# Two lines on when the last gate's steps are handed out: credit reset without pending work, and one more step between cast and sum

## The chip, the cores and the metric

The kernel runs on one core of a Trainium2 chip. The metric is the device time of one execution in microseconds (us). Of the engines, PE (TensorE) multiplies matrices, DVE (VectorE) and ACT (ScalarE) do element-wise work, POOL (GpSimd) does a few small operations, and SP (SyncE) issues the DMA transfers. Each engine works its own queue in order, and engines wait for one another by semaphores.

## The reference

One block of a diffusion transformer on 512 tokens of `x` and 256 of a context, width 1024, all in float32. Nine modulation vectors come from `c`, and three sublayers follow: a SwiGLU feed-forward (ffn1), a mixer of windowed attention and a gated scan, and a second SwiGLU feed-forward (ffn2). Each is normalized, shifted and scaled before, and gated behind. What matters here:

```python
mod = (silu(c) @ w_ada + b_ada).reshape(B, 9, 1, D)      # m[j] = mod[:, j]
h = ada_pre(x, norm_pre[2], m[6], m[7])
x = x + 0.5 * m[8] * rmsnorm(swiglu(h, ffn2_w_in, ffn2_w_out), norm_post[2])
```

`m[8] * norm_post[2] * 0.5` is called the last gate below. It is wanted only at the very end of ffn2, where the result is normalized and added.

## The kernel before, in words

Every matrix product is done in three passes: each operand is split into a rounded part (an ACT cast, line 65) and the remainder (a DVE subtraction, line 66), and PE multiplies high by high, low by high and high by low. So each weight tile costs an ACT cast and a DVE subtraction before PE can use all of it.

**ffn2** (`ffn7`) runs over 22 tiles j of 128 hidden columns. Tiles 0 and 1 are computed in the plain way (`std_tile`), tiles 2 to 21 by a scheme with seven products instead of eight: `weights(j)` loads two raw tiles U and G (512 KB each) through a pool of three buffers `wraw`, forms three sums on DVE (lines 408 to 411), and splits four stationary operands g0, g2, g1 and gc (`wh`/`wl`, three buffers, and `wch`/`wcl`, one). The seven products are twelve matmuls each, in the order A = g0, B = g0's other half, A = g2, C = g1, A += gc, C += g2, A += g1. Between uses, A and C are taken out of PSUM by ACT (lines 476, 483, 485, 492) and DVE (478, 487, 489). PE can start the last product of a tile only when DVE's line 487 has read A. Tiles are grouped into pieces of 1, 3, 3, 3, 3, 3, 2 and 4; after the first tile of a piece, PE multiplies the piece before it by the output weights (lines 71 to 74 with `woh`, the output phase).

**The modulation work** beside it is a list of generators, `background`. `mod_half` computes 512 columns of `silu(c) @ w_ada`: eight times it loads 256 KB of `w_ada` into `wa` (two buffers) and lets DVE multiply and add it into `macc` (lines 611 and 613), yielding its cost after each. Then it splits `macc` (the cast and remainder into `mx`, two buffers) and lets PE sum over the partitions with a stationary operand of ones (lines 622 and 623, an `aux` bank of PSUM). `mod_gate` does this for two halves, and behind each sum loads a row of `b_ada` and one of `norm_post` into the same `mx` buffers and combines them (lines 656 and 657).

**What hands the steps out** is `tick(n)` (line 294). It adds n to a credit, and runs steps of `background` while the credit is above zero; each step subtracts what it yields. ffn1 calls it 42 times with 4.2 (176.4 in all) and once with 1000 at its end. Its four generators yield 32, 64, 16 and 32, which is 144, so the credit stands at over 1000 when ffn2 begins. ffn2 puts the last gate's generator on the list at the end of tile 1 (line 1198) and calls `tick(1)` twice in each of the tiles 2 to 21.

The program text written this way is then put in a fixed order for each engine by the Tile framework's scheduler, which looks ahead by its own costs. So the order of the rows below is that of the built program, not that of the source.

Of the kernel before, what the change touches and what calls it, by code (L numbers as in the profile page):

```python
# [37 lines left out]
def view(ap, off, dims):  # L38

    return AP(ap.tensor, ap.offset + off, [ap.ap[0]] + [list(d) for d in dims])  # L40
# [3 lines left out]
def kernel(ctx: ExitStack, tc: tile.TileContext, i, out):  # L44
# [10 lines left out]
    def ps(tag="mm", shape=(P, 512)):  # L55
        return psum.tile(list(shape), F32, tag=tag, name=nm(tag), bufs=4)

    def ct(shape, tag, dt=F32, bufs=1, pool=None):
        return (pool or core).tile(list(shape), dt, tag=tag, name=nm(tag), bufs=bufs)

    def f32(ap):
        return ap.bitcast(F32)

    def split(hi, lo, src):
        nc.scalar.copy(hi, src)  # L65
        nc.vector.tensor_tensor(out=lo, in0=src, in1=f32(hi), op=ALU.subtract)  # L66
# [73 lines left out]
    def make_cols(n, v, shift, scale):  # L140

        a = ct([P, KD], f"colA{n}{v}")
        b = ct([P, KD], f"colB{n}{v}")
        jb, js = 3 * n, 3 * n + 1
        nc.vector.tensor_tensor(out=b, in0=shift, in1=vec[:, R_B + jb * KD:R_B + (jb + 1) * KD], op=ALU.add)
        nc.vector.tensor_tensor(out=a, in0=scale, in1=vec[:, R_B + js * KD:R_B + (js + 1) * KD], op=ALU.add)
        nc.vector.scalar_tensor_tensor(out=a, in0=a, scalar=1.0, in1=vec[:, R_PRE + n * KD:R_PRE + (n + 1) * KD],
                                       op0=ALU.add, op1=ALU.mult)
        mcol[n, v] = lambda k: (a[:, k:k + 1], b[:, k:k + 1])
# [65 lines left out]
    def rstd(z, n, scratch):  # L215

        ss = ct([P, 1], "ss", bufs=8)
        if isinstance(z, (list, tuple)):
            s2 = ct([P, 2], "ss2", bufs=4)
            for q, zz in enumerate(z):  # L220
                nc.scalar.activation(scratch[:, q * 512:(q + 1) * 512], zz, AF.Square, accum_out=s2[:, q:q + 1])
            nc.vector.tensor_tensor(out=ss, in0=s2[:, 0:1], in1=s2[:, 1:2], op=ALU.add)
        else:
            nc.scalar.activation(scratch, z, AF.Square, accum_out=ss)
        r = ct([P, 1], "rs", bufs=8)
        nc.gpsimd.tensor_scalar(ss, ss, 1.0 / n, EPS, ALU.mult, ALU.add)  # L226
        nc.gpsimd.tensor_tensor(out=r, in0=ss, in1=mhalf, op=ALU.pow)  # L227
        return r
# [61 lines left out]
    background = []  # L290

    credit = [0.0]

    def tick(n):

        credit[0] += n
        while background and credit[0] > 0:
            try:
                credit[0] -= next(background[0])
            except StopIteration:  # L300
                background.pop(0)
# [299 lines left out]
    with tc.tile_pool(name="f1", bufs=1, reuse_waits="tile") as f1:  # L601

        def mod_half(j, h, vs, pool):

            accs = [ct([P, 512], "macc", bufs=2, pool=pool) for _ in vs]
            for k in range(KD):
                w = ct([P, 512], "wa", bufs=2, pool=pool)
                nc.sync.dma_start(w, i["w_ada"][0, k * P:(k + 1) * P, j * D + h * 512:j * D + (h + 1) * 512])
                for v, a in zip(vs, accs):
                    if k == 0:  # L610
                        nc.vector.tensor_scalar(a, w, cs[:, v, k:k + 1], None, ALU.mult)
                    else:
                        nc.vector.scalar_tensor_tensor(out=a, in0=w, scalar=cs[:, v, k:k + 1], in1=a,  # L613
                                                       op0=ALU.mult, op1=ALU.add)
                yield len(vs)
            outs = []
            for v, a in zip(vs, accs):
                o = ps("aux")
                hi = ct([P, 512], "mx", F32R, bufs=2, pool=pool)
                lo = ct([P, 512], "mx", F32R, bufs=2, pool=pool)  # L620
                split(hi, lo, a)
                nc.tensor.matmul(o, lhsT=ones, rhs=hi, start=True, stop=False)
                nc.tensor.matmul(o, lhsT=ones, rhs=lo, start=False, stop=True)
                outs.append(o)
            return outs

        def mod_cols(n, vs, pool):
            cols = {(j, v): ct([P, KD], "mc", bufs=4, pool=pool) for j in range(2) for v in vs}
            for j in range(2):
                for h in range(2):  # L630
                    outs = yield from mod_half(3 * n + j, h, vs, pool)
                    for v, o in zip(vs, outs):
                        m = ct([P, 512], "mx", bufs=2, pool=pool)
                        nc.vector.tensor_tensor(out=m.rearrange("p (a b) -> p a b", b=P),
                                                in0=o.rearrange("p (a b) -> p a b", b=P),
                                                in1=view(ident, 0, [(0, 4), (1, P)]), op=ALU.mult)
                        nc.vector.tensor_reduce(out=cols[j, v][:, h * 4:(h + 1) * 4],
                                                in_=m.rearrange("p (a b) -> p a b", b=P), axis=AX.X, op=ALU.add)
            for v in vs:
                make_cols(n, v, cols[0, v], cols[1, v])  # L640

        def mod_gate(n, vs, w, pool):
            j = 3 * n + 2
            for v in vs:
                gg[n, v] = ct([P, D], "gg", bufs=3)
            for h in range(2):
                cols = slice(h * 512, (h + 1) * 512)
                outs = yield from mod_half(j, h, vs, pool)
                bb = ct([P, 512], "mx", bufs=2, pool=pool)
                b_, np_ = i["b_ada"], i["norm_post"]  # L650
                nc.sync.dma_start(bb, AP(b_.tensor, b_.offset + j * D + h * 512, [[0, P], [1, 512]]))
                gb = ct([P, 512], "mx", bufs=2, pool=pool)
                nc.sync.dma_start(gb, AP(np_.tensor, np_.offset + n * D + h * 512, [[0, P], [1, 512]]))
                for v, o in zip(vs, outs):
                    g = gg[n, v][:, cols]
                    nc.vector.tensor_tensor(out=g, in0=o, in1=bb, op=ALU.add)
                    nc.vector.scalar_tensor_tensor(out=g, in0=g, scalar=float(w), in1=gb, op0=ALU.mult, op1=ALU.mult)

        hh2 = ct([P, KD, TA], "hh", F32R)
        hl2 = ct([P, KD, TA], "hl", F32R)  # L660
        waiting = {}
        hts = []

        def post(t, o, n, v, w4, res):

            y = tok[t]
            scr = ct([P, D], "w4", bufs=4, pool=w4)
            for h in range(2):
                hc = slice(h * 512, (h + 1) * 512)
                nc.vector.tensor_tensor(out=y[:, hc], in0=y[:, hc], in1=o[h], op=ALU.add)  # L670
            r = rstd(y, D, ct([P, D], "am", mybir.dt.bfloat16, bufs=2, pool=w4))
            nc.vector.tensor_tensor(out=scr, in0=y, in1=gg[n, v], op=ALU.mult)
            nc.vector.scalar_tensor_tensor(out=y, in0=scr, scalar=r, in1=res, op0=ALU.mult, op1=ALU.add)
            return scr

        def last1(t, o):
            res = ct([P, D], "wraw", bufs=3)
            src = i["x"][0, t * P:(t + 1) * P, :] if t < NX else i["ctx"][0, (t - NX) * P:(t - NX + 1) * P, :]
            nc.sync.dma_start(res, src)
            scr = post(t, o, 0, 0 if t < NX else 1, f1, res)  # L680
            waiting[t] = pre_xn(t, scr)
            for s in sets:
                if t == s[-1]:
                    hts.append(make_hT(1, hh2, hl2, s, [waiting[q] for q in s], f1, tag="sg"))
            steps(hts, HT_STEPS.get(t, 0))

        for t in range(NT):
            tok[t] = ct([P, D], "tok", bufs=6)
        background += [mod_gate(0, (0, 1), 0.5, f1), mod_cols(1, (0, 1), f1),
                       mod_gate(1, (0,), 1.0, f1), mod_cols(2, (0,), f1)]  # L690
        first_w = []

        def final_pre():
            first_w.append(v_w(0))

        ffn(i["ffn1_w_in"][0], i["ffn1_w_out"][0], (hh, hl), GROUPS, NT, f1, PIECES, tok, last1,
            pre=pre1, ticks=4.2, final_pre=final_pre, order=ORDER)
        steps(hts, 1000)
# [223 lines left out]
    with tc.tile_pool(name="ma", bufs=1, reuse_waits="tile") as ma:  # L922
# [42 lines left out]
        vs = ct([P, NT, 2, 2, 64], "vs", F32R, pool=ma)  # L965
# [298 lines left out]
```

## Time and profile before

| | us |
|---|---|
| time, median of 3 runs (1508.75 to 1509.24) | 1508.85 |
| the profiled execution | 1511.06 |
| its span | 1509.3 |
| PE busy in the span | 1433.2 (95%) |
| DVE busy in the span | 984.5 (65%) |
| ACT busy in the span | 583.2 (39%) |

The span is what the trace covers, from its first instruction to its last. The profiled execution has 1.8 us around it. ffn1 fills about the first 610 us, and the mixer what lies between it and ffn2, whose first tiles begin at about 1130 us; tile 2 begins at 1152 us. A matmul's own duration in a timeline is longer than its distance to the next, since matmuls are pipelined; so a row of PE is read by its start.

### The profile page before, as it was taken

How to read it: one execution, taken by the hardware profiler on the slowest of the kernel's cores; microseconds unless marked ns; L12 is line 12 of the kernel's file. 1: busy time of each engine (PE TensorE's matmuls, PEld its weight loads, DVE VectorE, ACT ScalarE, POOL GpSimd, SP SyncE). 2: the span in 40 equal slices, each digit the busy share in tenths (PEclk: the TensorE clock that was granted, in tenths of full speed). 3: DMA queues.
4: the chain of work that ended last, by engine and by line, in shares of the span. 5: the costliest groups of instructions: out<-in, count | busy, mean ns of one | idle time of the engine just before them, and what ended most of it. 6: DMA issues, size and time to landing. Idle time of an engine off the chain costs nothing.

```text
span 1509.3 us, 22491 instructions
## 1 busy us (share of the span) xinstructions
PE 1433.2 (95%) x9064; PEld 1228.2 (81%) x9064; DVE 984.5 (65%) x1601; ACT 583.2 (39%) x973; POOL 59.2 (4%) x87
## 2 busy tenths in 40 slices
PE   6999999999999999899999899999996699999997
PEld 3688888888788887789889677788776599999996
DVE  6866564666654334856687679743468677787785
ACT  6532121212121122532333578632256244454442
POOL 3200000000000000200001100000010000000001
PEclk9999999999999999999999999999999799999999
DMA  9554332455551111221121111133316333333311
GB/s 309 177 187 132 105 113 80 121 162 152 169 154 42 56 43 56 80 85 43 43 68 52 56 43 57 32 99 100 117 46 213 108 102 106 101 101 109 95 47 56
DMA packets 177904, 151.57 MB, mean 100 GB/s; under 512 B 6408, under 2 KB 152328, under 8 KB 177800
## 3 DMA queue, kind: packets, MB, share of 16 engines
q1 hardware_dynamic: 177800, 150.14, 32.8%
q8 instruction: 71, 1.16, 0.3%
q14 instruction: 33, 0.27, 0.1%
HBM read 148.02 MB, written 2.10 MB: 99 GB/s over the span
## 4 chain that ended last, share of the span: by engine, by line
PE 68%; issue 15%; DVE 7%; DMA 4%; ACT 3%; POOL 2%; SPq 0%; DVEq 0%; POOLq 0%; ACTq 0%
PE mm L71 17%; PE mm L74 16%; PE mm L72 16%; DMA wa<-w_ada 3%; PE mm L421 2%; PE mm L422 2%; PE mm L423 2%; PE aux L421 2%; PE aux L422 2%; PE aux L423 2%; DVE macc L613 1%; POOL rs L227 1%; DVE wl L66 1%; PE aux L1044 1%; POOL ss L226 1%
## 5 line engine op out<-in xcount | busy, mean ns | idle before, releaser
L71 PE MATMUL mm<-hh,wh 128*128 128x512 f32 (+1 forms) x1128 | 388.9, 346 | 0.5 <-ACT sg L332 0.2
L72 PE MATMUL mm<-hl,wh 128*128 128x512 f32 (+1 forms) x1128 | 368.0, 343 | 0.0
L74 PE MATMUL mm<-hh,wl 128*128 128x512 f32 (+1 forms) x1128 | 325.5, 346 | 0.7 <-DVE wl L66 0.7
L66 DVE TENSOR_TENSOR wl<-wraw,wh 128x1024 fp32r<-128x1024 f32 (+1 forms) x159 | 189.5, 1196 | 179.2 <-ACT wh L65 178.0
L65 ACT CAST wh<-wraw 128x1024 fp32r<-128x1024 f32 (+1 forms) x159 | 163.1, 1028 | 355.5 <-PE mm L72 230.6
L71 PEld LDWEIGHTS mm<-hh,wh 128*128 128x128 f32 x1128 | 212.1, 188 | 46.0 <-ACT gg L909 0.7
L72 PEld LDWEIGHTS mm<-hl,wh 128*128 128x128 f32 x1128 | 212.4, 188 | 27.2 <-DVE hl L541 0.8
L74 PEld LDWEIGHTS mm<-hh,wl 128*128 128x128 f32 x1128 | 185.6, 190 | 8.9 <-DVE wl L66 1.1
L71 PE MATMUL mm<-woh,acth 128*128 128x512 f32 x420 | 164.5, 392 | 1.9 <-DVE am L334 1.1
L72 PE MATMUL mm<-wol,acth 128*128 128x512 f32 x420 | 164.0, 391 | 0.0
L613 DVE SCALAR_TENSOR_TENSOR macc<-wa,cs,macc 128x512 f32<-128x512 f32 x140 | 101.8, 749 | 61.7 <-DMA wa<-w_ada 60.7
L74 PE MATMUL mm<-woh,actl 128*128 128x512 f32 x420 | 130.6, 390 | 0.0
L65 ACT CAST woh<-w 128x1024 fp32r<-128x1024 f32 x42 | 44.3, 1055 | 153.5 <-PE mm L74 150.7
L71 PEld LDWEIGHTS mm<-woh,acth 128*128 128x128 f32 x420 | 78.9, 188 | 20.0 <-DVE am L334 2.0
L74 PEld LDWEIGHTS mm<-woh,actl 128*128 128x128 f32 x420 | 78.8, 188 | 16.6
L72 PEld LDWEIGHTS mm<-wol,acth 128*128 128x128 f32 x420 | 78.9, 188 | 15.6
L369 DVE TENSOR_TENSOR tok<-tok,mm 128x512 f32<-128x512 f32 x96 | 61.5, 683 | 34.5 <-PE mm L74 34.4
L421 PE MATMUL mm<-hh,wh 128*128 128x256 f32 x240 | 68.1, 284 | 2.0 <-ACT up L476 2.0
L421 PE MATMUL aux<-hh,wh 128*128 128x256 f32 x240 | 69.1, 288 | 0.0
L422 PE MATMUL aux<-hl,wh 128*128 128x256 f32 x240 | 69.0, 287 | 0.0
L423 PE MATMUL aux<-hh,wl 128*128 128x256 f32 x240 | 68.9, 287 | 0.0
L423 PE MATMUL mm<-hh,wl 128*128 128x256 f32 x240 | 67.8, 283 | 0.1
(342 smaller groups left out, 2478.5 us busy)
## 6 DMA issues: line engine op xcount, KB each, us to landing
wraw<-ffn_w_in SPq DMA_DIRECT2D x88, 512.0 KB, 4.0
wa<-w_ada SPq DMA_DIRECT2D x128, 256.0 KB, 3.2
w<-ffn_w_out SPq DMA_DIRECT2D x44, 512.0 KB, 4.3
wraw<-mix_w_in SPq DMA_DIRECT2D x42, 512.0 KB, 3.7
tok<-w_ada SPq DMA_DIRECT2D x16, 256.0 KB, 5.6
wraw<-w_out SPq DMA_DIRECT2D x8, 512.0 KB, 4.3
tok<-x SPq DMA_DIRECT2D x4, 512.0 KB, 8.2
wraw<-x SPq DMA_DIRECT2D x4, 512.0 KB, 3.3
```

What stands on the lines that cost most here:

```text
L65: nc.scalar.copy(hi, src)
L66: nc.vector.tensor_tensor(out=lo, in0=src, in1=f32(hi), op=ALU.subtract)
L71: nc.tensor.matmul(o, lhsT=sh, rhs=mh, start=start, stop=False)
L72: nc.tensor.matmul(o, lhsT=sh, rhs=ml, start=False, stop=False)
L74: nc.tensor.matmul(o, lhsT=sl, rhs=mh, start=False, stop=stop)
L226: nc.gpsimd.tensor_scalar(ss, ss, 1.0 / n, EPS, ALU.mult, ALU.add)
L227: nc.gpsimd.tensor_tensor(out=r, in0=ss, in1=mhalf, op=ALU.pow)
L369: nc.vector.tensor_tensor(out=y, in0=y, in1=o[h], op=ALU.add)
L421: nc.tensor.matmul(o, lhsT=wk, rhs=mh, start=first and k == 0, stop=False, skip_group_check=True)
L422: nc.tensor.matmul(o, lhsT=wk, rhs=ml, start=False, stop=False, skip_group_check=True)
L423: nc.tensor.matmul(o, lhsT=wl[:, k0 + k, :], rhs=mh, start=False, stop=k == H4 - 1, skip_group_check=True)
L613: nc.vector.scalar_tensor_tensor(out=a, in0=w, scalar=cs[:, v, k:k + 1], in1=a, op0=ALU.mult, op1=ALU.add)
```

## The change

Two places. In `tick`, the credit is set to zero whenever the list of pending work is empty, so that what ffn1 did not use is not carried to ffn2. In `mod_half`, where one vector is computed and not two (`len(vs) == 1`), one more step of cost 1 is yielded between the split and the sum by PE. That concerns the last gate, and in ffn1 the two generators with one vector (`mod_gate(1, ...)` and `mod_cols(2, ...)`, six halves).

```diff
     def tick(n):
 
-        credit[0] += n
+        credit[0] = credit[0] + n if background else 0.0
         while background and credit[0] > 0:
...
                 split(hi, lo, a)
+                if len(vs) == 1:
+                    yield 1
                 nc.tensor.matmul(o, lhsT=ones, rhs=hi, start=True, stop=False)
                 nc.tensor.matmul(o, lhsT=ones, rhs=lo, start=False, stop=True)
```

From line 622 on, a line of the new kernel has a number two higher. In the rows of the built programs a name carries a buffer number, and an arrow points from what is read to what is written.

On PE, in tile 2 of ffn2, the rows before from the last matmuls of the product gc (`wch`) on; `ones` is the sum over partitions of a half of the last gate, `aux_10489` the second product B:

```order
L421 MATMUL mm_10488<-hh_9717,wch_10472 128x256
L422 MATMUL mm_10488<-hl_9718,wch_10472 128x256
L423 MATMUL mm_10488<-hh_9717,wcl_10473 128x256
L622 MATMUL aux_10412<-mx_10413,ones_62 128x512
L623 MATMUL aux_10412<-mx_10414,ones_62 128x512
L622 MATMUL aux_10450<-mx_10451,ones_62 128x512
L623 MATMUL aux_10450<-mx_10452,ones_62 128x512
L421 MATMUL aux_10489<-hh_9717,wh_10467 128x256
L422 MATMUL aux_10489<-hl_9718,wh_10467 128x256
```

The same place now, from the last matmuls of gc on:

```order
L421 MATMUL mm_10416<-hh_9717,wch_10400 128x256
L422 MATMUL mm_10416<-hl_9718,wch_10400 128x256
L423 MATMUL mm_10416<-hh_9717,wcl_10401 128x256
L421 MATMUL aux_10448<-hh_9717,wh_10406 128x256
L422 MATMUL aux_10448<-hl_9718,wh_10406 128x256
L423 MATMUL aux_10448<-hh_9717,wl_10407 128x256
L421 MATMUL aux_10448<-hh_9717,wh_10406 128x256
L422 MATMUL aux_10448<-hl_9718,wh_10406 128x256
L423 MATMUL aux_10448<-hh_9717,wl_10407 128x256
```

The four matmuls with `ones` are gone from tile 2; B now stands ahead of gc, and behind gc comes C += g2 of the same tile.

They now stand in tile 6 (the first half; `wh_11035` is g0 of tile 6, `wh_11046` its g2) and, for the second half, in tile 11 behind an output phase:

```order
L423 MATMUL aux_11057<-hh_9717,wl_11036 128x256
L421 MATMUL aux_11057<-hh_9717,wh_11035 128x256
L422 MATMUL aux_11057<-hl_9718,wh_11035 128x256
L423 MATMUL aux_11057<-hh_9717,wl_11036 128x256
L624 MATMUL aux_11026<-mx_11027,ones_62 128x512
L625 MATMUL aux_11026<-mx_11028,ones_62 128x512
L421 MATMUL mm_11056<-hh_9717,wh_11046 128x256
L422 MATMUL mm_11056<-hl_9718,wh_11046 128x256
```

On DVE, behind the split of tile 2's weights, before (`macc` is the last gate's accumulator, `wraw_10590` U of tile 3):

```order
L408 TENSOR_TENSOR wc_10598<-wraw_10590,wraw_10592 128x512
L409 TENSOR_TENSOR wraw_10592<-wraw_10592 128x512
L613 SCALAR_TENSOR_TENSOR macc_10387<-wa_10400,cs_75,macc_10387 128x512
L66 TENSOR_TENSOR wcl_10600<-wc_10598,wch_10599 128x512
L613 SCALAR_TENSOR_TENSOR macc_10387<-wa_10403,cs_75,macc_10387 128x512
L613 SCALAR_TENSOR_TENSOR macc_10387<-wa_10406,cs_75,macc_10387 128x512
L613 SCALAR_TENSOR_TENSOR macc_10387<-wa_10409,cs_75,macc_10387 128x512
L66 TENSOR_TENSOR mx_10414<-macc_10387,mx_10413 128x512
L611 TENSOR_SCALAR macc_10425<-wa_10426,cs_75 128x512
L613 SCALAR_TENSOR_TENSOR macc_10425<-wa_10429,cs_75,macc_10425 128x512
```

And now, where `wraw_10524` is U of tile 3:

```order
L489 TENSOR_TENSOR up_10418<-up_10418,aux_10448 128x256
L409 TENSOR_TENSOR wraw_10526<-wraw_10526 128x512
L66 TENSOR_TENSOR wcl_10534<-wc_10532,wch_10533 128x512
L493 TENSOR_TENSOR up_10418<-sg_10449,up_10418 128x512
L410 TENSOR_TENSOR wraw_10524<-wraw_10524,wraw_10526 128x512
L613 SCALAR_TENSOR_TENSOR macc_10387<-wa_10672,cs_75,macc_10387 128x512
L66 TENSOR_TENSOR actl_10518<-up_10418,acth_10517 128x512
L411 TENSOR_TENSOR wraw_10524<-wraw_10524 128x512
L478 TENSOR_TENSOR up_10551<-up_10551,aux_10550 128x256
L613 SCALAR_TENSOR_TENSOR macc_10387<-wa_10729,cs_75,macc_10387 128x512
L66 TENSOR_TENSOR wl_10540<-wraw_10524,wh_10539 128x1024
```

Before, the sixteen multiplications by `w_ada` stood almost one behind another ahead of tile 2's line 478. Now they stand singly or in twos between the tiles' own work, the first five ahead of tile 3's remaining splits and the last one ahead of tile 6's first sum.

On SP, the transfers of `w_ada` (`wa`) and of the weights (`wraw`) moved in the same way. Now, from the load of G of tile 3 (`wraw_10526`) on:

```order
L96 DMA wraw_10526<-ffn_w_in 128x8x128
L608 DMA wa_10672<-w_ada 128x512
L96 DMA wraw_10675<-ffn_w_in 128x8x128
L608 DMA wa_10729<-w_ada 128x512
L345 DMA w_1989_11675<-ffn_w_out 128x1024
L608 DMA wa_10893<-w_ada 128x512
L608 DMA wa_10950<-w_ada 128x512
L96 DMA wraw_10677<-ffn_w_in 128x8x128
L96 DMA wraw_10896<-ffn_w_in 128x8x128
```

## Rows read from the trace of the kernel before

**Rows 1.** The page: granted TensorE clock in 40 slices, tenths.
```profile
PEclk9999999999999999999999999999999799999999
```

**Rows 2.** Windows: us, busy PE, PEld, DVE, ACT, POOL, PEclk, DMA.
```profile
1150.00:1160.00 10.00, 7.32 (x46) 6.11 (x45) 8.65 (x10) 6.15 (x10) 0.00 (x0) 1.00 0.80 243
1160.00:1170.00 10.00, 0.00 (x0) 0.00 (x0) 4.99 (x7) 1.15 (x2) 0.00 (x0) 0.75 0.78 247
1170.00:1180.00 10.00, 1.52 (x2) 0.57 (x2) 4.72 (x8) 0.09 (x1) 0.00 (x0) 0.50 0.59 182
...
1190.00:1200.00 10.00, 10.00 (x75) 9.80 (x75) 7.91 (x12) 5.69 (x9) 0.00 (x0) 0.89 0.09 22
```

**Rows 3.** Waits of PE, 1100 to 1290 us: total us, times, longest us.
```profile
PE aux L622 <- ACT mx L65: 24.4, 2, 14.2
PE mm L421 <- ACT up L476: 2.0, 1, 2.0
...
PE mm L421 <- ACT up L483: 0.5, 1, 0.5
```

**Rows 4.** Chain of waits, 1140 to 1200 us: start us, us, what.
```profile
1159.91 5.11 DMA wa<-w_ada
...
1171.69 3.93 DMA mx<-norm_post
```

**Rows 5.** Windows in the steady part of ffn2.
```profile
1280.00:1320.00 40.00, 40.00 (x293) 38.05 (x292) 32.41 (x46) 18.36 (x30) 0.00 (x0) 1.00 0.39 117
```

**Rows 6.** Timeline of PE: start us, us, what; idle before it in brackets.
```profile
1152.09 0.28 PE L421 MATMUL mm<-hh,wh 128*128 128x256 f32 x1
...
1153.40 0.28 PE L423 MATMUL mm<-hh,wl 128*128 128x256 f32 x1
...
1170.14 0.79 PE L622 MATMUL aux<-mx,ones 128*128 128x512 f32 x1 [10.21 <-ACT mx L65]
1170.87 0.80 PE L623 MATMUL aux<-mx,ones 128*128 128x512 f32 x1
...
1187.15 0.41 PE L421 MATMUL aux<-hh,wh 128*128 128x256 f32 x1
...
1192.26 0.28 PE L421 MATMUL mm<-hh,wh 128*128 128x256 f32 x1
```

**Rows 7.** Timeline of DVE in the same stretch.
```profile
1155.06 2.36 DVE L66 TENSOR_TENSOR wl<-wraw,wh 128x1024 fp32r<-128x1024 f32 x2
...
1161.23 0.69 DVE L408 TENSOR_TENSOR wc<-wraw,wraw 128x512 f32<-128x512 f32 x1 [1.36 <-DMA wraw<-ffn_w_in]
```

**Rows 8.** Timeline of the SP queue: when transfers were issued.
```profile
1156.31 0.38 SPq L96 DMA_DIRECT2D wraw<-ffn_w_in  x1
```

**Rows 9.** Groups of instructions by line, 1200 to 1480 us: busy us, mean ns.
```profile
L66 DVE TENSOR_TENSOR wl<-wraw,wh 128x1024 fp32r<-128x1024 f32 x54 | 65.7, 1225 | 14.6 <-ACT wh L65 14.6
...
L65 ACT CAST wh<-wraw 128x1024 fp32r<-128x1024 f32 x53 | 55.6, 1050 | 24.9 <-PE aux L422 17.1 <-DVE wraw L411 4.2 <-PE mm L422 3.0
...
L411 DVE TENSOR_TENSOR wraw<-wraw 128x512 f32<-128x512 f32 x18 | 12.4, 687 | 0.2
...
L478 DVE TENSOR_TENSOR up<-up,aux 128x256 f32<-128x256 f32 x19 | 8.0, 419 | 1.3
```

**Rows 10.** Groups by line in the first 620 us.
```profile
L613 DVE SCALAR_TENSOR_TENSOR macc<-wa,cs,macc 128x512 f32<-128x512 f32 x126 | 91.3, 749 | 53.4 <-DMA wa<-w_ada 52.7
```

**Rows 11.** DMA issues, 1075 to 1215 us: KB each, median us to landing.
```profile
wraw<-ffn_w_in SPq DMA_DIRECT2D x13, 512.0 KB, 4.3
...
wa<-w_ada SPq DMA_DIRECT2D x16, 256.0 KB, 4.0
```

**Rows 12.** Waits of PE in the first 620 us, longest total first.
```profile
PE aux L552 <- DVE tok L548: 5.0, 5, 1.8
...
PE mm L71 <- DVE am L334: 1.1, 2, 0.9
```

## The prediction

> **What bounds the kernel now.** I read the page first. PE is busy for 95% of the span, and its granted clock is above nine tenths of 2.4 GHz in every slice but one, the one that begins at 1170 us (thirty-one slices of 37.7 us) [rows 1]. Windows of that stretch show where: from 1160 to 1170 us PE does nothing, from 1170 to 1180 us 1.5 us, and the clock falls to 0.50, which is 1.2 GHz, and is back only in the window after 1190 us [rows 2]. DVE is half idle there too, so no engine is the bound. The waits of PE give the name: two waits of the matmul with `ones` for the cast of `macc`, 24.4 us together, and two of 2.0 and 0.5 us for the tile's own evacuations [rows 3]. What is behind the cast is seen in the chain: loads of `w_ada`, one after another, since there are two buffers, and the load of a constant (5.1 and 3.9 us are examples of the two) [rows 4]. So in tile 2 of ffn2 PE stands behind two sums whose sixteen loads have just been asked for, and four products of the tile that do not need them stand behind the sums. After that, PE is full: in 40 us of the steady part it is busy 40, and DVE 32.4 [rows 5]. Time given back to PE at tile 2 is therefore time given back at the end, unless a new wait takes it.
>
> **What goes.** (a) The sums leave tile 2: 24.4 us of waiting [rows 3]. (b) The other two waits, 2.5 us, are reopened, since product B now stands before A = g2; their new size is below. (c) The half clock. The four `ones` matmuls follow each other at 0.73 us [rows 6]; at 2.4 GHz I take half, so 4 x 0.36 = 1.4 us. The 24 matmuls from 1187.15 to 1192.26 us took 5.11 us; eleven steps from 1152.09 to 1153.40 us give 0.12 us each, so 24 take 2.9 us, a saving of 2.2 us [rows 6]. Together 24.4 + 2.5 + 1.4 + 2.2 = 30.5 us.
>
> **What comes.** The sixteen multiplications, four casts and remainders, and the gate's four combinations are not fewer; they move into tiles 2 to 11, where PE works and DVE has little to spare.
>
> Tile 2. PE starts at 1152.09, as before; DVE's order up to the split of g1 is the same and ends at 1155.06 + 2.36 = 1157.42 us [rows 7]. A = g0 and B are 24 matmuls, 2.9 us, so PE is at A = g2 at 1155.0; before, it began that at 1155.7, and had to wait about 0.3 us more for the remainder of g2. I take 0.9 us. Line 487 stands behind one short line, two multiplications and two large splits, 4.4 us together by the durations below, so it ends at about 1162, when PE has just done the products ahead of the last one. No further wait counted.
>
> Tile 3. G of tile 3 is issued at 1156.31 [rows 8] and was used at 1161.23 [rows 7]; its place in SP's queue is unchanged, behind transfers that wait for the same DVE instructions. Then DVE decides. Between the split of tile 2's g1 and the end of tile 3's line 411 the new order has fifteen instructions: two of 128x1024 at 1.22 us, seven of 128x512 at 0.69, three of 128x256 at 0.42 [rows 9] and three multiplications of 0.75 [rows 10]: 2.4 + 4.8 + 1.3 + 2.2 = 10.8 us, or 9.8 with the starts some 0.07 us ahead of the ends before them. So line 411 ends at 1167.2 to 1168.2, and the cast of g2 (1.05 us [rows 9]) at 1168.3 to 1169.3. PE has 84 matmuls of tile 2 and 24 of tile 3 until then, 13.0 us, plus 0.9 of waiting: it arrives at 1166.0. That is a wait of 2.3 to 3.3, and since the remainder follows the cast by a DVE step of 1.2, about 0.8 more less what the high parts cover. I take 3.3 us. Then G of tile 4 can be loaded only when g2 of tile 3 is split, takes 4.3 us [rows 11], and line 408, which waits for it, now stands ahead of line 487, for which PE waits: 0.3 us by the same count.
>
> Tile 4. The same two, smaller, because some matmuls of the output phase now stand between its products: 0.8 us at g2 and 0.4 at line 487. Behind it PE has some 15 us of output phase, in which DVE needs little, and catches up.
>
> Later. The rows of 1280 to 1320 show 7.6 us of DVE idle in 40 [rows 5]; the rest of the multiplications (under 5 us) and the combinations fall into such stretches. The constants' loads wait for the sum by PE, and DVE waits for them with line 487 of tile 6 behind. The load took 3.9 us [rows 4], the combination 0.7, and PE has four products (48 x 0.12 = 5.8 us) before it needs line 487. So it is hidden, by about 0.5 us; without that cover it costs up to 2 us. In tile 11 the sum stands ahead of the tile's first product, and the cover is six products. I take 0.5 us for all of this.
>
> ffn1. Six more steps make 150 against a credit of 176.4, so all is still done there; five of six pairs of `ones` move 48 matmuls or more later on PE. PE's waits in ffn1 name no `ones` matmul, from 5.0 us in total down [rows 12]. Cost nothing; PE itself hides it. A gain is excluded, as there is no such wait to win back, and a loss I bound at 1 us.
>
> Sum: new waits 0.9 + 3.6 + 1.2 + 0.5 = 6.2 us, so 30.5 - 6.2 = 24.3 us saved. The profiled execution took 1511.06 us with a span of 1509.3, 2.2 us above the median of the runs; the saving is one of PE waiting within the span and is taken off the median: 1508.85 - 24.3 = 1484.5 us.
>
> Bounds: with tile 2's 0.9 alone the saving is 29.6, and the time 1479. If the wait in tile 3 lets the clock fall again, it costs the 2.2 us of (c) once more. Rows show a wait of 2.0 us after which the clock stayed at 1.00, and one of 10.2 us with 0.50 behind it [rows 2, 3]; 3.3 us lies between, nearer to the first, so I take none. The Trainium skill ("TensorE: Matmul & The Clock Gate", Part 1, The HAM clock gate) says that an idle PE goes back to half rate and must be kept busy for some time before it is given the full rate. The trace agrees with both halves, and by that rule taken strictly the sum would be 1486.7.
>
> **Rivals.** First, DVE does not hide the gate's work. For it: in the three tiles between output phases DVE's own work, about 9.9 us a tile, is already as long as PE's 84 matmuls, 10.1. Against it: the output phases, and that DVE is held by PE's release of the weight buffers (17.1 us of the cast's idle time [rows 9]), so it runs ahead. If all of it lands on the path, it is 16 x 0.75 + 6 x 0.69 = 16.1 us, beside tile 2's 0.9: 30.5 - 17.0 = 13.5 us saved, 1495 us.
>
> Second, slower than before: the multiplications block DVE. One that waits for its load holds everything behind it on DVE, line 487 too, and PE can cover only one product of 1.4 us. If each load is issued so late that its full 4.0 us [rows 11] is waited for, this is 16 x 2.6 = 42 us, 12 more than saved: 1521 us. It decides from an average wait of 1.4 + 29.6 / 16 = 3.3 us a step. Against it: in ffn1, where the steps are spread in this way, 126 multiplications waited 52.7 us in all, 0.42 each [rows 10], and PE did not wait for it [rows 12]. There a tick hands out 4.2 of credit, here 1, so the loads are asked for less densely now. The Trainium skill (same page, "Architectural detail", the paragraph on engine queue depths) states that ACT and DVE are strictly first in, first out, which is what makes this possible. The trace agrees: from 1160 us on DVE is half idle [rows 2] while work of tile 3 stands behind the loads.
>
> Third, the change does not do what it says: PE waits as long for something else, as G of tile 3, which landed only at about 1161. But from there to tile 3's first use of it the count above has 7 us, not 30, and the order shows no sum in the tiles 2 to 5. It would give 1508.
>
> **Chances.** The forecast, with a saving of 19 to 30 us: 0.80. DVE in the way, 8 to 19 saved: 0.13. Blocked and slower: 0.03. No change: 0.02. The remaining 0.02 lie beyond 30 us saved. The range that holds 8 in 10 reaches from the lower bound, 1479, to 1493, some way into the first rival. A measurement of this kernel can tell a change of 0.2%, 3 us, from none. Faster by more than that 0.95, within it 0.02, slower 0.03.
>
> **What would show it.** In the profile after, the slice of the clock at about 1170 us is full or nearly so; the waits of PE name no `ones` matmul above 1 us; the largest new wait is that of A = g2 in tile 3 for line 65 or 66, 2 to 4 us at about 1166; the chain goes through PE there and no longer through the loads of `w_ada`. PE's windows from 1200 us on are as full as before, some 24 us earlier. I am wrong if PE's waits between tiles 3 and 11 add up to more than 10 us, if DVE shows waits for `wa` above 2 us with line 487 behind them, or if ffn1 ends later.

## The result and the profile after

| | before | after |
|---|---|---|
| time, median (range, runs), us | 1509.05 (1508.75 to 1509.34, 4) | 1486.75 (1484.94 to 1488.53, 4) |
| ratio, 95% interval | | 0.9852 [0.9835, 0.9869] |
| the profiled execution, us | 1511.06 | 1484.94 |
| its span, us | 1509.3 | 1483.2 |
| first to last matmul of `woh` by `acth` in ffn2, us | 353.5 | 328.0 |

The change saves 22.3 us by the medians. The last row of the table is a yardstick for ffn2 that I use throughout, since what lies ahead of ffn2 differs by some us from run to run. It is read from the view of line 71, whose row says when the first and the last of its matmuls started; of before and of after:

```profile
L71 PE MATMUL mm<-woh,acth x168: 388/389/397, 1146.6 to 1500.1; 128*128 128x512 f32 x168
```

```profile
L71 PE MATMUL mm<-woh,acth x168: 388/389/398, 1145.9 to 1473.9; 128*128 128x512 f32 x168
```

The granted clock on the page of after (answers to [rows 1]) has no slice below nine tenths at the place; the 8 is in the mixer. In the windows (columns as in [rows 2]) PE is idle for 2.5 us in ten at most, DVE is nearly full, and the clock stays at 1.00:

```profile
PEclk9999999999999999999999989999999999999999
```

```profile
1150.00:1160.00 10.00, 10.00 (x78) 9.56 (x77) 9.80 (x14) 6.86 (x11) 0.00 (x0) 1.00 0.87 271
1160.00:1170.00 10.00, 7.51 (x60) 7.08 (x60) 9.58 (x15) 5.64 (x9) 0.00 (x0) 1.00 0.56 178
1170.00:1180.00 10.00, 9.74 (x75) 8.88 (x74) 9.13 (x16) 5.34 (x10) 0.00 (x0) 1.00 0.52 164
1180.00:1190.00 10.00, 9.47 (x70) 8.82 (x70) 8.79 (x15) 2.95 (x7) 0.00 (x0) 1.00 0.63 189
```

PE's waits from 1130 to 1300 us (as in [rows 3]: us in total, times, longest) name no `ones` matmul:

```profile
PE mm L421 <- ACT wh L65: 2.2, 2, 2.0
PE mm L421 <- DVE sg L487: 2.1, 2, 1.5
PE aux L421 <- ACT wh L65: 0.4, 1, 0.4
```

The timeline of PE places them, one window of it after another: A = g2 of tile 3, C = g1 of tile 3 (for the cast of g1), line 487 of tile 4, the first sum in tile 6 (it waits for nothing), line 487 of tile 6.

```profile
1166.81 0.38 PE L421 MATMUL mm<-hh,wh 128*128 128x256 f32 x1 [2.05 <-ACT wh L65]
...
1167.76 0.38 PE L421 MATMUL aux<-hh,wh 128*128 128x256 f32 x1 [0.45 <-ACT wh L65]
...
1186.55 0.38 PE L421 MATMUL mm<-hh,wh 128*128 128x256 f32 x1 [0.53 <-DVE sg L487]
```

```profile
1215.78 0.40 PE L624 MATMUL aux<-mx,ones 128*128 128x512 f32 x1
1216.02 0.39 PE L625 MATMUL aux<-mx,ones 128*128 128x512 f32 x1
1216.25 0.28 PE L421 MATMUL mm<-hh,wh 128*128 128x256 f32 x1
...
1222.10 0.28 PE L422 MATMUL mm<-hl,wh 128*128 128x256 f32 x1
1223.90 0.39 PE L421 MATMUL mm<-hh,wh 128*128 128x256 f32 x1 [1.52 <-DVE sg L487]
1224.12 0.28 PE L422 MATMUL mm<-hl,wh 128*128 128x256 f32 x1
```

Two things are seen beside the waits. The `ones` matmuls now follow each other at 0.24 and 0.23 us, against 0.73 before [rows 6]. The half clock is only a part of those 0.73: the second of a pair reads the remainder, and DVE had that ready at 1170.12 + 0.69 = 1170.81 us, where PE started at 1170.87. From the timeline of DVE before:

```profile
1170.12 0.69 DVE L66 TENSOR_TENSOR mx<-macc,mx 128x512 fp32r<-128x512 f32 x1 [0.68 <-ACT mx L65]
```

And a wait costs more than its bracket: from 1222.10 to 1223.90 are 1.80 us where 0.12 is usual, and the next step takes 0.22, so 1.78 us are lost where 1.52 is shown, 0.26 more.

The chain of waits in the same stretch (as [rows 4]) no longer holds loads of `w_ada`; the load of G of tile 4 is in it, released by the split of tile 3's g2:

```profile
1165.72 1.05 ACT wh L65
1166.80 1.24 DVE wl L66
1168.05 4.50 DMA wraw<-ffn_w_in
```

### The profile page after: what moved, and what is told of

It is laid out like the page before. It is cut to its first block, busy times and chain, and to the rows that moved or that the text cites. A ratio compares the mean times of both kernels' runs of the same rounds, so it can differ in the third digit from the quotient of the medians.

```text
span 1483.2 us, 22466 instructions
## 1 busy us (share of the span) xinstructions
PE 1428.8 (96%) x9064; PEld 1227.1 (83%) x9064; DVE 982.1 (66%) x1601; ACT 583.2 (39%) x973; POOL 59.0 (4%) x87
## 4 chain that ended last, share of the span: by engine, by line
PE 70%; issue 16%; DVE 7%; ACT 3%; DMA 2%; POOL 2%; DVEq 0%; POOLq 0%; ACTq 0%; SPq 0%
PE mm L71 18%; PE mm L74 18%; PE mm L72 18%; PE mm L421 2%; PE mm L423 2%; PE mm L422 2%; PE aux L421 2%; PE aux L422 2%; PE aux L423 2%; PE aux L1046 1%; POOL rs L227 1%; DVE wl L66 1%; DMA mx<-b_ada 1%; DMA wa<-w_ada 1%; POOL ss L226 1%
## 5 line engine op out<-in xcount | busy, mean ns | idle before, releaser
L422 PE MATMUL mm<-hl,wh 128*128 128x256 f32 x240 | 67.8, 283 | 0.0
```

The source lines that it names most:

```text
L422: nc.tensor.matmul(o, lhsT=wk, rhs=ml, start=False, stop=False, skip_group_check=True)
```

## The experiments

All are compared with the kernel before on the same chip (medians of before: 1508.1 us for e1 to e4, 1509.8 for e5 to e8, 1507.91 for e9, e10 and e12). "Stretch" is the yardstick above, from one profile each.

| | time, us (range) | ratio [95%] | stretch, us |
|---|---|---|---|
| e1 reset alone | 1485.46 (1484.46 to 1488.98) | 0.9855 [0.9841, 0.987] | 329.1 |
| e2 late sum, no reset | 1491.42 (1491.05 to 1492.41) | 0.989 [0.9873, 0.9906] | 333.6 |
| e3 half pace | 1487.44 (1483.99 to 1488.92) | 0.9861 [0.9846, 0.9876] | 330.0 |
| e4 constants early | 1484.54 (1483.24 to 1485.35) | 0.9844 [0.983, 0.9859] | 325.8 |
| e5 no gate | 1476.49 (1475.11 to 1478.06) | 0.9786 [0.977, 0.9801] | 320.0 |
| e6 reset, constants early | 1481.92 (1481.08 to 1484.44) | 0.9824 [0.9807, 0.9841] | 326.3 |
| e7 gate on POOL | 1494.42 (1492.97 to 1495.17) | 0.9902 [0.9884, 0.992] | 338.4 |
| e8 step alone | 1508.72 (1506.53 to 1510.65) | 0.9995 [0.9985, 1.0006] | 352.4 |
| e9 late gate | 1478.6 (1477.26 to 1480.58) | 0.9806 [0.9792, 0.9819] | 322.4 |
| e10 loads by POOL's queue | 1481.98 (1480.49 to 1482.99) | 0.9826 [0.9812, 0.984] | 325.3 |
| e12 changed kernel again | 1486.53 (1484.79 to 1487.68) | 0.9853 [0.9839, 0.9868] | 329.4 |

**Which of the two edits does it: e1 and e8.** e1 is before with the reset alone, e8 with the added step alone.

```diff
-        credit[0] += n
+        credit[0] = credit[0] + n if background else 0.0
```

> The credit reset alone, without the extra step between cast and sum. Theory (the gain is that the sums no longer stand on PE's queue ahead of tile 2's products): the reset does all of it, so 1483 to 1487 us, ratio to before 0.983 to 0.985, no wait of a ones matmul. Here the first sum stands at the start of tile 6, two products earlier than with the extra step, so line 487 of tile 6 has 2.9 us more of cover and the 1.5 us wait of the changed kernel there should be gone: about 1.5 us faster than the changed kernel. Rival (the extra step is needed, since without it the sum is reached before its cast and remainder are done): a wait of a ones matmul of 1 to 3 us twice, 1489 to 1492 us.

> The added step alone, without the reset. Theory: the credit of over 1000 that ffn1 leaves hands out every step in the first tick, whatever their number; so both sums stand in tile 2 as before, PE waits about 24 us at them, and the time is that of before, 1507 to 1510. Rival: the added step alone moves the sum behind other products of the tile; then the wait is 20 us or less, and the time 1505 or less.

The reset alone gives the whole gain, the step alone nothing: e8's PE still waits 22.2 us at two `ones` matmuls. What I expected of e1's tile 6 was half wrong: of the 1.52 us there 0.79 was left, and 1.05 came in a later tile.

```profile
PE aux L624 <- ACT mx L65: 22.2, 2, 14.6
```

```profile
PE mm L421 <- DVE sg L487: 2.2, 3, 1.0
PE mm L421 <- ACT wh L65: 2.0, 1, 2.0
```

**Is it the place of the sums: e2.** The credit of before, but a costly step between cast and sum, so that the eight multiplications of the first half are handed out at once and its sum is put off; those of the second half come one a tick behind it.

```diff
                 split(hi, lo, a)
+                if late:
+                    yield late
...
+                outs = yield from mod_half(j, h, vs, pool, (1035.4, 4)[h] if n == 2 else 0)
```

> The credit of before is kept, so the eight multiplications of the gate's first half are all handed out in tile 2's first tick; only the sum on PE is put off, by a step whose cost uses up the credit, to about tile 7, and the second half comes one step a tick behind it. Theory (only the sum's place on PE matters): 1483 to 1488 us, ratio about 0.985, no wait of a ones matmul. Rival (what PE waited for is the burst of loads and multiplications, through DVE): waits of line 421 for DVE or ACT of 10 us or more in tiles 2 and 3, about 1497 us.

Neither figure was met; it came between. With the sums put off, 353.5 - 333.6 = 19.9 us of the stretch are won. The other 5.6 us have more than one cause. In e2 six multiplications stand on DVE between the split of tile 2's g1 and tile 3's line 411, against three in after, two of them behind loads, and PE waits 4.38 us there, with a clock of 0.50 to 0.53 from 1170 to 1176 us. And of the 4.1 us at line 487, 1.44 and 2.17 us come in later tiles, where DVE stood for the constants' load (as in after, with 1.52 and 0.24 us). How the 5.6 us divide is not shown.

```profile
PE mm L421 <- ACT wh L65: 4.4, 1, 4.4
PE mm L421 <- DVE sg L487: 4.1, 3, 2.2
```

**What is left: e3, e4, e6.** e3 hands out half as much a tick (`ticks=0.5`). e4 loads the gate's constants ahead of its steps, into buffers of their own; e6 is e4 without the added step.

```diff
-                outs = yield from mod_half(j, h, vs, pool)
-                bb = ct([P, 512], "mx", bufs=2, pool=pool)
+                if n == 2:
+                    both = ct([P, D], "gg", bufs=3)
+                    bb, gb = both[:, :512], both[:, 512:]
...
+                if n == 2:
+                    outs = yield from mod_half(j, h, vs, pool)
```

> The changed kernel with half the credit in ffn2, one step every second tick. The built order keeps the multiplications on DVE at the same places (tiles 2 to 5) and moves only the sums, to behind the output phase ahead of tile 11, and to tile 18. Theory (the changed kernel's 1.5 us wait for line 487 in tile 6 is DVE standing for the constants' load behind the sum): that wait is gone, as no sum stands in tile 6; the 2.5 us in tile 3 stay; 1.5 us less than the changed kernel, 1483 to 1487, if the place in tile 18 costs nothing. Rival (line 487 is late in tile 6 because DVE is behind from tiles 3 to 5): the 1.5 us stay, time as the changed kernel.

> The changed kernel with the gate's two constants of each half loaded ahead of its multiplications, into buffers of their own that are free in ffn2. Sums and multiplications stay where the changed kernel has them. Theory (constants' load behind the sum holds DVE): the wait for line 487 in tile 6 falls from 1.5 us to under 0.3, the waits in tiles 3 and 4 (2.5 and 0.7 us) stay: 1483 to 1487 us, about 1.5 less than the changed kernel. Rival (DVE is behind by its own work): the wait in tile 6 stays at 1 us or more and the time is that of the changed kernel.

> The reset alone, without the added step, and with the gate's constants loaded ahead of its steps into buffers of their own. Theory: the sum's place decides, not the added step, and the waits in tile 6 and behind come from the constants' load that holds DVE; so no wait of PE for line 487 above 0.5 us behind tile 5, and the time is that of the changed kernel with early constants, 1483 to 1486. Rival: the added step is needed to keep the cast ahead of the sum; then PE waits 0.5 us or more at a matmul with ones, and the time is 1486 or more.

e3 gains nothing: the multiplications stay where they were and only the sums move (to tiles 11 and 18); that the scheduler takes them as early as it can is my reading, not shown. The wait in tile 6 is gone, but that in tile 3 is 2.91 us here, and one of 0.78 us appears at 1305.60. e4 settles tile 6: with the constants there in time, PE waits nowhere behind tile 4. In after, SP and DVE themselves show it: the second `ones` matmul starts at 1216.02, the first constant is issued at 1216.21, DVE stands 1.47 us for it, and line 487 behind. The timelines of SP and of DVE:

```profile
1216.21 0.34 SPq L653 DMA_DIRECT2D mx<-b_ada  x1
```

```profile
1219.46 0.69 DVE L409 TENSOR_TENSOR wraw<-wraw 128x512 f32<-128x512 f32 x1
1221.62 0.69 DVE L658 TENSOR_TENSOR gg<-aux,mx 128x512 f32<-128x512 f32 x1 [1.47 <-DMA mx<-b_ada]
1222.23 0.68 DVE L410 TENSOR_TENSOR wraw<-wraw,wraw 128x512 f32<-128x512 f32 x1
1222.83 0.69 DVE L659 SCALAR_TENSOR_TENSOR gg<-gg,mx 128x512 f32<-128x512 f32 x1
1223.43 0.41 DVE L487 TENSOR_TENSOR sg<-sg,mm 128x256 f32<-128x256 f32 x1
```

```profile
PE mm L421 <- ACT wh L65: 2.0, 1, 2.0
...
PE mm L421 <- DVE sg L487: 0.8, 1, 0.8
```

e6 shows no wait at a sum either, so the added step isn't needed for the cast. Its stretch is e4's within 0.5 us; that its time is 2.6 us lower, on another chip, comes from ahead of ffn2, where ffn1's end scatters by 2 to 3 us between profiles. What the added step costs there is bounded by e8: with the step alone the time is at most 1.0006 of before's, 0.9 us more.

**What the gate's work costs at all: e5.** The gate is left out of ffn2, and a constant 1 stands in its place.

```diff
-            background.append(mod_gate(2, (0,), 0.5, f2))
+            gg[2, 0] = ct([P, D], "gg", bufs=3)
+            nc.gpsimd.memset(gg[2, 0], 1.0)
```

> The changed kernel without the last gate in ffn2: the sixteen loads of w_ada, the multiplications, casts, sums by PE and combinations are left out, and the gate's value is a constant 1 (so this part of the computation is missing). It is the floor for what the gate's work still costs once the sums are spread. Theory: the waits of PE that are left in tiles 3, 4 and 6 (about 4.8 us in the trace of the changed kernel) come from the gate's steps on DVE, so PE waits under 1 us in all from tile 2 to tile 6, and the time is some 4 to 6 us under the changed kernel's, about 1481; the four matmuls with ones themselves are about 1 us of it. Rival: tile 3's wait of 2 to 2.5 us is the tiles' own start-up (G of tile 3 arrives late, then a chain of four sums, cast and remainder). Then 1.5 us or more stays at A = g2 of tile 3, and the time is 1483 to 1484.

PE waits nowhere in ffn2 from tile 2 on, tile 3 included, so the rival of a start-up of the tiles' own falls. The price is larger than I expected, 8.0 us of stretch (9.4 against e12, the same program as after). It adds up, nearly, from the rows of after: waits of 2.05 + 0.45 + 0.18 + 0.53 + 1.52 + 0.24 (tile 11) = 5.0 us, six times 0.26 for the restarts, 1.6, and two pairs of sums at 0.47, 0.9; together 7.5.

**Which resource: e7, e10.** e7 is e4 with the sixteen multiplications given to POOL. e10 is e6, with them on DVE, but with their loads issued from POOL's queue.

```diff
...
+                    elif j == 8:
+                        nc.gpsimd.tensor_scalar(w, w, cs[:, v, k:k + 1], None, ALU.mult)
+                        nc.gpsimd.tensor_tensor(out=a, in0=a, in1=w, op=ALU.add)
...
```

```diff
-                nc.sync.dma_start(w, i["w_ada"]...
+                (nc.gpsimd if j == 8 else nc.sync).dma_start(w, i["w_ada"]...
```

> The changed kernel with early constants, and with the last gate's sixteen multiplications on POOL, as two instructions each but for the first of a half. In the kernel before one addition of 128x512 on POOL took 1.6 us, so 32 instructions or so are about 50 us, spread over the tiles 2 to 11. Theory: DVE has 12 us less to do there, the waits at A = g2 of tile 3 (2.05 and 0.45 us) and at tile 4 (0.8) go down to under 1 us together, and the time is 2 to 3 us less than with early constants alone, about 1482. Rival: POOL and DVE hold each other up, so that lines 408 to 411 take clearly more than 0.69 us while POOL works; then the waits stay or grow, and the time is 1485 or more.

> As e6, with the gate's sixteen loads of w_ada issued from POOL's queue and not from SP's. Theory (queue): in tiles 3 and 4 SP holds the load of the next weights behind loads of w_ada that wait for a buffer (in the trace of the changed kernel two of w_ada from 1164.45 to 1166.97 us, the weights behind at 1168.05); with a queue of their own the weights land earlier, line 408 waits under 0.3 us for them in tiles 4 and 5, and the wait at line 487 (0.9 us) is gone, so 1 to 2 us are won against e6. Rival (work): DVE's own instructions set the pace there; then the waits stay within 0.5 us of those of e6, and so does the stretch from first to last output matmul (326.3 us).

e7 went the rival's way and further. While POOL works, some of DVE's instructions are longer; by groups from 1150 to 1220 us (busy us, mean ns, idle before), after and then e7:

```profile
L66 DVE TENSOR_TENSOR wl<-wraw,wh 128x1024 fp32r<-128x1024 f32 x15 | 17.9, 1221 | 1.9 <-ACT wh L65 1.9
...
L411 DVE TENSOR_TENSOR wraw<-wraw 128x512 f32<-128x512 f32 x5 | 3.4, 685 | 0.0
...
L487 DVE TENSOR_TENSOR sg<-sg,mm 128x256 f32<-128x256 f32 x4 | 1.7, 416 | 0.7 <-PE mm L423 0.7
```

```profile
L66 DVE TENSOR_TENSOR wl<-wraw,wh 128x1024 fp32r<-128x1024 f32 x12 | 17.5, 1464 | 1.2 <-ACT wh L65 1.1
...
L411 DVE TENSOR_TENSOR wraw<-wraw 128x512 f32<-128x512 f32 x4 | 4.2, 1062 | 0.0
...
L410 DVE TENSOR_TENSOR wraw<-wraw,wraw 128x512 f32<-128x512 f32 x3 | 2.1, 685 | 0.0
...
L487 DVE TENSOR_TENSOR sg<-sg,mm 128x256 f32<-128x256 f32 x3 | 1.2, 412 | 0.0
```

Line 487, which reads one operand out of PSUM, is not longer, though it ran in the midst of POOL's work. The Trainium skill ("GPSIMD Engine Reference", 1. Specifications) says that POOL's way into SBUF is shared with VectorE and contended by VectorE's instructions with two inputs in SBUF. Lines 66, 411 and 487 agree with it; line 410, with two inputs in SBUF too, took 685 ns, so not every such instruction was held.

And a second thing, which neither theory had: POOL took 3.8 us for a step (2.28 + 1.50 by its groups' means), so its loads waited long for a buffer, on the queue on which the weights stand behind them. SP held two loads of `w_ada` for 3.33 us, later two for 5.63 us; the weights went out only then, and line 408 waited for them 2.57 and 5.56 us:

```profile
1153.19 3.33 SPq L610 DMA_DIRECT2D wa<-w_ada  x2
1156.61 0.39 SPq L96 DMA_DIRECT2D wraw<-ffn_w_in  x1
...
1168.95 5.63 SPq L610 DMA_DIRECT2D wa<-w_ada  x2
1174.67 0.39 SPq L96 DMA_DIRECT2D wraw<-ffn_w_in  x1
```

```profile
1160.95 0.69 DVE L408 TENSOR_TENSOR wc<-wraw,wraw 128x512 f32<-128x512 f32 x1 [2.57 <-DMA wraw<-ffn_w_in]
...
1178.66 0.69 DVE L408 TENSOR_TENSOR wc<-wraw,wraw 128x512 f32<-128x512 f32 x1 [5.56 <-DMA wraw<-ffn_w_in]
```

```profile
1163.13 0.38 PE L421 MATMUL mm<-hh,wh 128*128 128x256 f32 x1 [3.33 <-DVE sg L487]
...
1181.44 0.58 PE L421 MATMUL aux<-hh,wh 128*128 128x256 f32 x1 [7.91 <-ACT sg L485]
```

PE's first wait there, 3.33 us, is that of line 487 behind the held line 408: the prediction's second rival, DVE blocked by a queue, in small. The second, 7.91 us, ended with ACT: its line 485 stood behind the cast of `macc`, which waited for POOL's last addition. From the timeline of ACT:

```profile
1180.50 0.62 ACT L65 CAST mx<-macc 128x512 fp32r<-128x512 f32 x1 [9.15 <-POOL macc L616]
1181.03 0.37 ACT L485 COPY sg<-aux 128x256 f32<-128x256 f32 x1
```

e10 speaks against such a block in after: with a queue of its own for the loads the time is e6's, the stretch 1.0 us shorter, and line 408 still waits 1.18 and 1.08 us for its weights. Neither of the figures ahead of it was met: the wait in tile 3 fell from 2.05 to 1.04 us, two of 0.63 and 0.54 us at line 487 are left. And it is not the queue alone, since the built order of DVE is another too (the remainder of the first half's `macc` at 1180.67 us, in e6 at 1173.65). The chain of after above shows why SP is not what is waited for there: the weights' load at 1168.05 starts when the split of g2 frees its buffer (1166.80 + 1.24 = 1168.04), not when SP is free, which it was from 1166.97 us on. A kernel with four buffers for the gate's loads (e11) has no time: its pool takes 84 KB a partition, and 76.4 are left.

**Is it the place: e9.** e9 is e6, but the multiplications read a copy of `cs` that can't be there before the first result of an output phase is in `yacc`, and a step of cost 9 stands ahead of them. So they are held back.

```diff
...
+                        yield 9
+                        late = ct([P, 1, KD], "cl", pool=pool)
+                        nc.gpsimd.tensor_scalar(late[:, 0, :], yacc[0][:, :KD], 0.0, None, ALU.mult)
+                        nc.gpsimd.tensor_tensor(out=late[:, 0, :], in0=late[:, 0, :], in1=cs[:, 0, :], op=ALU.add)
```

> The reset with early constants (as in e6), and the gate's multiplications held back to the tiles 6 to 8: they read a copy of the vector cs that POOL makes only when the first output phase of yacc is done. Theory: what is left of the gate's price, about 6 us against the kernel without the gate, is paid only because its loads and multiplications fall into the tiles 2 to 4, where the weights of the next tile are late; moved behind, DVE has 7.6 us idle in 40. So no wait of PE above 0.5 us in the tiles 2 to 5, the stretch from the first output matmul to the last (326.3 us in e6, 320.0 without the gate) takes 321 to 323, and the time is 1477 to 1480. Rival: the gate's work costs about the same wherever it stands, since the waits for the weights' loads move with it; then PE waits 2 us or more at A = g2 or at line 487 in the tiles 6 to 9, and the stretch takes 325 or more.

> The changed kernel itself once more, on the same chip as the three others, to compare them with it: 1485 to 1488, and 328 us from the first output matmul to the last. If the reset alone with early constants is better than it, as e6 had it, the kernels of this call that are built on e6 and lose nothing are 2 us or more below it.

As the theory had it: two waits of 0.5 us in all, the stretch 322.4 us, 2.4 above the kernel without the gate and 3.9 below e6, where the same work stands in the earlier tiles. It is the best time of all kernels with the gate, 8 us below the changed kernel on the same chip (1478.6 against 1486.53 us). The multiplications stand in the output phase behind tile 4 (the first at 1186.94 us) and in tiles 5 to 7 (the last at 1229.93), somewhat ahead of the tiles 6 to 8 that I had expected. There they are hidden, and in tiles 2 to 4 the same sixteen were not. Their loads moved with them, so e9 does not tell DVE's time from that of the transfers.

```profile
PE mm L421 <- DVE sg L487: 0.5, 2, 0.3
```

## Why the prediction was right

Forecast 1484.5 us in 1479 to 1493, measured 1486.75; the mechanism and the place of the new waits were as written; some of the sizes were not. Term by term, with the measured value from the profile of after (of e12 in brackets):

| term | predicted | measured |
|---|---|---|
| (a) waits of the sums | 24.4 gone | gone |
| (b) reopened waits | 2.5 gone | gone |
| (c) half clock, four `ones` matmuls | 1.4 gone | 1.52 + 1.32 before, 2 x 0.47 now: 1.9 gone |
| (c) half clock, 24 matmuls | 2.2 gone | clock 1.00 (0.50 for a while in tile 3) |
| tile 2, A = g2 | 0.9 | none (none) |
| tile 3 | 3.3 + 0.3 | 2.05 + 0.45 (2.86 + 0.27) |
| tile 4 | 0.8 + 0.4 | 0.18 + 0.53 (0.51) |
| later | 0.5 | 1.52 + 0.24 (1.33 + 0.57) |
| restarts of PE | not counted | 1.0 gone, 1.6 new (six waits at 0.26, an estimate) |

The restarts' 1.0 is a remainder: from 1153.40 to 1192.26 us PE in before took 38.86 us for 49 steps from one matmul to the next, 5.9 us at 0.12, and the four `ones` matmuls; the waits, the 2.2 us of half clock and the `ones` (2.8) are 31.9, and 1.0 is left. Measured: 24.4 + 2.5 + 1.9 + 2.2 + 1.0 = 32.0 gone, 5.0 + 1.6 = 6.6 new, 25.4 us saved; the difference of the stretches is 353.5 - 328.0 = 25.5. So close a fit is in part luck, since e12, the same program as after, has 329.4. That the prediction's 24.3 came so near is luck too: its errors cancel.

- *Tile 2 and tile 3 were taken too high.* In before DVE had stood 1.23 us at 1152.26 for the first load of `w_ada`; in after that load was there (in e12 it was waited for 0.65 us), and DVE was 1.6 us earlier from 1153 us on, of which 0.7 are that all of ffn2 began earlier. I had left DVE where it was. So line 411 of tile 3 ended at 1165.6, not at 1167.2 to 1168.2; the count of fifteen instructions held. The 0.3 us that I gave to line 487 of tile 3 were not there; the 0.45 us are the cast of g1, which I had not counted.
- *The step that failed is "later".* I let the combination be hidden "by about 0.5 us, without that cover up to 2 us". The cover was not there: PE needed line 487 at about 1222.4 and got it only at 1223.90, 1.52 us. I had taken 3.9 us for the load and 0.7 for what follows. The load was issued at 1216.21 and DVE went on at 1221.62, 5.4 us later; then both lines of the combination, line 410 and line 487 itself took until 1223.84, 2.2 us. e4 shows the cause: with the two loads moved this wait is gone, and those of tiles 3 and 4 stay.
- *Term (c) was right for the 24 matmuls only.* For the `ones` matmuls I halved 0.73 us, but the second of a pair had waited for the remainder (above). And the wait of 10.2 us, which I cite from [rows 3], is in [rows 6].
- *How large the gain is depends on the pair of runs.* The profiled before had a stretch of 353.5 us, e8, which has the same two sums in tile 2, 352.4; after had 328.0 and e12 329.4. Such pairs differ by 23.0 to 25.5 us, and the medians by 22.3 and 21.4. The pair of the table is an extreme one: its before took longer than the four runs listed, its after is the fastest of its four. What is left of 1 to 2 us I can't place.
- *The first rival* (DVE does not hide the gate's work, 1495) was partly true, and the price was the start-up's: e5 puts all that the gate costs at 8.0 us, e9 at 2.4 in better tiles. *The second* needs slow steps, as in e7, where PE waited 3.33 us in this way. *The third* falls with e8 against e1: the sums moved, and the wait with them.
- ffn1 at nothing: no `ones` matmul waits there after, and e8's time leaves room for 0.9 us at most, if its ffn2 costs what that of before does.

## What to carry to other kernels

Work that is handed out by a credit must not take over what earlier work left unused: here 24 us of waiting came from a leftover of over 1000, and one line takes it back. Where such work should go is read from the windows of the engine that does it: the gate's work, with its constants there in time, cost 326.3 - 320.0 = 6.3 us in the start-up of the pipeline (e6) and 2.4 us behind the next output phase (e9). And a load that is asked for only when a result is there can hold an engine that works in order: here DVE stood 1.47 us for it, and PE 1.52 us for what stood behind; with the constants asked for ahead (e4) both waits are gone.

## What was not expected of the hardware

The clock did not follow the length of PE's wait alone. Two windows of 2 us each behind a wait of 2.05 us in e1, and the same with the same wait in after (columns as in [rows 2]):

```profile
1166.00:1168.00 2.00, 1.85 (x8) 1.56 (x8) 2.00 (x3) 1.54 (x2) 0.00 (x0) 0.50 0.48 132
1168.00:1170.00 2.00, 2.00 (x15) 2.00 (x15) 1.97 (x4) 0.37 (x1) 0.00 (x0) 0.74 0.81 233
```

```profile
1166.00:1168.00 2.00, 0.74 (x4) 0.54 (x4) 1.83 (x3) 2.00 (x3) 0.00 (x0) 1.00 0.42 132
1168.00:1170.00 2.00, 2.00 (x18) 1.99 (x18) 2.00 (x3) 1.03 (x2) 0.00 (x0) 1.00 0.54 179
```

In e1 the clock fell to 0.50 (1.2 GHz) and was back at 1.00 from 1170 us on; in after it stayed at 1.00. e4 and e6 kept 1.00 as well, behind the same 2.05 us. In e12, the same program as after, it fell to 0.50 in one such window, behind a wait of 2.86 us. The rule that the prediction cites from the Trainium skill ("TensorE: Matmul & The Clock Gate", Part 1, The HAM clock gate) is thus borne out by e1 and e12 and not by after, e4 and e6, for the same product of the same tile; of my "nearer to the first, so I take none" the most that can be said is that one profile of the changed kernel agrees and one does not. In e7 some of DVE's instructions were longer while POOL worked, line 411 in the mean by half, 685 to 1062 ns, which the trace of before could not show, as POOL was idle in this stretch.
